# Memory attention in a decoder-trunk kernel: query weights loaded in one go, sample tokens queried with the second chunk, and their attention moved between the other slots

## The chip, the cores and the metric

The kernel runs as one program on 1 core of one Trainium2 chip. The metric is the device time of one execution in microseconds (us). The engines are TensorE (PE, with its weight loads, PEld), VectorE (DVE), ScalarE (ACT), GpSimd (POOL) and SyncE (SP), whose queue issues nearly all the DMAs here.

## The reference

One inference step of a decoder layer for 1,024 prompt tokens and 8 x 4 = 32 sample tokens, in three residual parts: a mixer (gated MLP beside latent attention), attention into a memory, and a gated feed-forward part with a short convolution. The change lies in the second part:

```python
def mem_attend(h, mk, mv, w_mq, g_mq, w_mo):
    n, t, _ = h.shape
    q = rms_norm((h @ w_mq).reshape(n, t, MEM_HEADS, MEM_HEAD_DIM), g_mq)
    s = jnp.einsum('nthd,nmhd->nhtm', q, mk.astype(q.dtype)).astype(jnp.float32) * (MEM_HEAD_DIM ** -0.5)
    p = jax.nn.softmax(s, axis=-1).astype(q.dtype)
    o = jnp.einsum('nhtm,nmhd->nthd', p, mv.astype(q.dtype)).reshape(n, t, MEM_WIDTH)
    return o @ w_mo
```

There are 4 heads of 128 and 256 memory tokens. The prompt attends to keys and values that the kernel computed earlier (`o_mk`, `o_mv`). Each of the 8 samples attends to its own cached keys and values, `mkT` and `mv` (8 tiles of 512 KB each), which are read from memory.

## The kernel before

Products are made three times over: an operand is split into a high and a low part (`split`: an ACT cast, then a DVE subtraction, lines 201 and 202, or 205 and 208 with a gain), and `mm3` (line 186) adds high x high, high x low and low x high.

**Output projection** (`out_proj`). Eight row tiles `m` by three token chunks of 384, 384 and 288. The last chunk holds 256 prompt tokens and the 32 sample tokens and runs two tiles late. Each result is added to the residual on DVE (line 1768), stored, split into `xh` and `xl` (the operand of the next stage) and squared (ACT), and the squares are summed on POOL (line 1801). After the last tile, `token_roots` makes the inverse token norms `r3` from the sums, by some twenty small DVE instructions per chunk.

**Memory attention** (`mem_attention`). PE's order is written out by hand (`manual_schedule`). For the other engines a scheduler makes the order when the program is built; at run time every engine takes its instructions strictly in that order. The work of PE is a list of slots `s`:

- `project(h)` loads the query weights of head `h` (`w_mq`, 512 KB) into one of three `raw` buffers, scales them on POOL (line 1576) and splits them: heads 0 to 2 into one of three pairs that the output projection also uses, head 3 into a pair of its own (`wxh`, `wxl`). `memory()` loads `o_mk` and `o_mv` through the same `raw` buffers and splits them into `kh`, `kl`, `vh` and `vl`. In the code the order is: project 0, slot 0, memory, project 1, slot 1, project 2, and so on.
- Slots 0 to 15 run over four chunks of 256 prompt tokens with four heads each. A slot is `scores` of five slots ago, `query`, `values` of seven slots ago and `trans` of six slots ago, each named for what it multiplies or transposes. A query writes one of two banks `b`; a bank is free again when DVE has made `ql` from it. The fourth chunk has 288 columns: the sample tokens come last, and the query makes `qs` (DVE) and `qm` (POOL) from them. Every fourth slot ends with `square_sums`, and `roots` follows one slot later.
- Slots 16 to 22 run the pipeline empty and hold the samples' attention: `sample_scores` with three, three and two samples in slots 16 to 18 (line 1930), a softmax, `sample_trans` in slot 19, `sample_values` with four samples each in slots 21 and 22 (line 1966), `sample_out` at the end. `ahead` (slots 19 to 22) makes the first pieces of the output product with `w_mo`. Keys and values of the samples go through five buffers `skT`; five keys are loaded ahead, and each further load is issued when a buffer has been used. The masks `pm` for the values are POOL products (line 1949) with four buffers.

After slot 15 the space of `xh` and `xl` is given to other tiles: four residual tiles (line 2029) and the sums of feed-forward weights (line 2241) are loaded there. After slot 22 comes the rest of the output product (tile `y`) and the feed-forward part.

Of the kernel before, what the change touches and what calls it, by code (L numbers as in the profile page):

```python
# [13 lines left out]
P = 128  # L14
# [140 lines left out]
class Net:  # L155
# [1648 lines left out]
    def mem_attention(self, xh, xl, r3):  # L1804
# [30 lines left out]

        def query(h, c):
            o, n = 256 * c, 288 if c == 3 else 256
            ps = bank("b", 2)[:, :n]
            self.mm3(ps, [(w[h][0][:, k], w[h][1][:, k]) for k in range(8)], [(xh[:, k, o : o + n], xl[:, k, o : o + n]) for k in range(8)])
            qsq[h] = self.t(p, [P, 288], F32, f"qsq{h}", 1)[:, :n]  # L1840
            nc.scalar.activation(qsq[h], ps, AF.Square)
            self.split(qh[:, h, o : o + n], ql[:, h, o : o + n], ps, gmq)
# [4 lines left out]
        rows = self.t(p, [P, 384], F32, "rows", 1)  # L1847

        def square_sums(c):

            n = 288 if c == 3 else 256
            st = bank("st", 1)[:, :n]
            for h in range(4):
                nc.tensor.matmul(st[32 * h : 32 * h + 32], self.ones[:, :32], qsq[h], start=True, stop=True)
            if c == 3:
                nc.gpsimd.memset(rows[:, n:], 1.0)
            nc.scalar.copy(rows[:, :n], st)

        def roots(c):

            m, t = 3 if c == 3 else 2, slice(2 * c, 9 if c == 3 else 2 * c + 2)
            st = bank("st", 1)[:, : m * P].rearrange("p (k n) -> p k n", k=m)
            for k in range(m):
                nc.tensor.transpose(st[:, k], rows[:, k * P : k * P + P], self.ident)
            x = self.t(p, [P, 3, 4], F32, "rsq", 2)[:, :m]
# [6 lines left out]

        units = [(h, g) for g in range(4) for h in range(4)]

        def scores(i):
            h, g = units[i]
            ps = bank("s", 2).rearrange("p (e n) -> p e n", e=2)
# [3 lines left out]
            pr[i] = self.t(p, [P, 2, 256], F32, "pr", 3)  # L1881
            self.softmax(p, pr[i], ps, P, rm[:, 2 * g : 2 * g + 2, h])

# [9 lines left out]
        def values(i):  # L1893
            h, g = units[i]
            th, tl = ts.pop(i)
# [28 lines left out]
        def sample_scores(b0, b1):  # L1924
# [7 lines left out]
            if b1 == NB:  # L1932
                sc = self.t(pe, [P, 1], F32, "sc")
                for h in range(4):
                    nc.gpsimd.tensor_copy(sc[heads[h]], rm[:NS, 8, h : h + 1])
                sample["p"] = self.t(pe, [P, 1, 256], F32, "pf", 1)
                self.softmax(pe, sample["p"], sample["s"].unsqueeze(1), P, sc)

        def sample_trans():
            tp = bank("st", 1)[:, :256].rearrange("p (k n) -> p k n", k=2)  # L1940
            for k in range(2):
                nc.tensor.transpose(tp[:, k], sample["p"][:, 0, k * P : k * P + P], self.ident)
            pT = self.t(pe, [P, 1, 256], F32, "pf", 1).rearrange("p a (k n) -> p (a k) n", k=2)
            nc.vector.tensor_copy(pT, tp)
            sample["m"] = []
            for b in range(NB):
                pm = self.t(pe, [P, 2, 4, NS], F32, "pm", 4)
                sample["m"].append(pm)
# [3 lines left out]
                )  # L1952
                if b < 4:
                    f()
# [3 lines left out]
        def sample_values(b0):  # L1958
            if b0 == 0:
                sample["o"] = bank("sx", 1)[:, :P]  # L1960
            so = sample["o"]
            for b in range(b0, b0 + 4):
                v, pm = skv.pop(0), sample["m"][b]
                for k in range(2):
                    for h in range(4):
                        nc.tensor.matmul(
                            so[heads[h]], pm[:, k, h], v[:, k, h * P : h * P + P], start=b + k == 0, stop=b == NB - 1 and k == 1
                        )
                if b0 == 0:
                    sample_load(1)  # L1970
                    sample["m", b + 4]()
            if b0:
                sample["d"] = self.t(pe, [P, 1, 256], F32, "pf", 1)[:, 0, :P]
                nc.scalar.copy(sample["d"], so)
# [25 lines left out]
        form = lambda p, h, n: ops[h].__setitem__(n, [self.t(p, [P, 4, QT], FR, f"{n}{h}{q}") for q in "hl"])  # L2000
        E = mybir.EngineType
        with tc.manual_schedule(engines={E.PE}):
            for s in range(16):
                if s < 4:
                    project(s)
                slot(s)
                if s == 0:
                    self.token_roots(p, bank("sx", 1), r3, 2)
                    nc.vector.tensor_copy(rt, r3)
                    memory()  # L2010
                if s == 7:
                    sample_load(5)
            self.close("x")
# [578 lines left out]
```

## Time and profile before

| | us |
|---|---|
| Runs shown: median (lowest to highest of 3) | 1833.23 (1832.74 to 1837.23) |
| The profiled execution: its own time | 1834.78 |
| Span of the profiled execution | 1833.0 |
| PE busy in the span | 1795.4 (98%) |
| DVE, ACT, POOL busy | 1353.7 (74%), 919.8 (50%), 713.2 (39%) |

The mean clock granted to TensorE was 0.992 of full speed. Times are counted from the start of the span. The output projection ends at about 981 us, the slots 0 to 15 lie between 983 and 1065 us, the slots 16 to 22 between 1065 and 1109 us, and the feed-forward part takes the rest. In a row of the timeline the columns are start, duration, engine, line, operation, tiles, count, and in brackets how long the engine was idle before and who ended that. A row of the chain of waits has start, duration and what. A row of the table of stretches has the stretch, its length, the busy time of each engine (with the number of instructions), the granted clock, the share of the DMA engines and GB/s.

### The profile page before, as it was taken

How to read it: one execution, taken by the hardware profiler on the slowest of the kernel's cores; microseconds unless marked ns; L12 is line 12 of the kernel's file. 1: busy time of each engine (PE TensorE's matmuls, PEld its weight loads, DVE VectorE, ACT ScalarE, POOL GpSimd, SP SyncE). 2: the span in 40 equal slices, each digit the busy share in tenths (PEclk: the TensorE clock that was granted, in tenths of full speed). 3: DMA queues.
4: the chain of work that ended last, by engine and by line, in shares of the span. 5: the costliest groups of instructions: out<-in, count | busy, mean ns of one | idle time of the engine just before them, and what ended most of it. 6: DMA issues, size and time to landing. Idle time of an engine off the chain costs nothing.

```text
span 1833.0 us, 39420 instructions
## 1 busy us (share of the span) xinstructions
PE 1795.4 (98%) x14259; PEld 1702.0 (93%) x14259; DVE 1353.7 (74%) x2805; ACT 919.8 (50%) x1921; POOL 713.2 (39%) x865
## 2 busy tenths in 40 slices
PE   9999999999999999999998989999999999999999
PEld 8999777779999999998897979999999999999999
DVE  7864767657678777788644676898888888888664
ACT  7435676766556555556433555533333333444442
POOL 1021655534445454553032021377667776400000
PEclk9999999999999999999998999999999999999999
DMA  8102354558776766663654065222222222495242
GB/s 322 46 18 72 123 164 127 167 181 232 211 208 183 202 183 189 181 194 124 186 156 163 13 215 174 83 82 79 95 72 71 82 71 82 144 331 163 83 149 78
DMA packets 153188, 261.19 MB, mean 142 GB/s; under 512 B 20897, under 2 KB 97538, under 8 KB 152994
## 3 DMA queue, kind: packets, MB, share of 16 engines
q1 hardware_dynamic: 152130, 257.63, 45.1%
q8 instruction: 113, 1.85, 0.4%
q10 hardware_dynamic: 864, 1.05, 0.2%
q14 instruction: 81, 0.66, 0.1%
HBM read 212.79 MB, written 45.82 MB: 141 GB/s over the span
## 4 chain that ended last, share of the span: by engine, by line
PE 80%; DVE 4%; ACT 2%; DMA 2%; issue 1%; SPq 0%; POOL 0%; DVEq 0%; ACTq 0%; POOLq 0%
PE s L186 22%; PE d L186 12%; PE b L186 8%; PE F L186 7%; PE X L186 7%; PE E L186 7%; PE A L186 3%; PE y L186 2%; PE o L1047 2%; PE o L1538 2%; PE tp L1032 1%; PE tp L186 1%; PE s L1423 1%; PE b L1606 1%; PE tp L985 1%
## 5 line engine op out<-in xcount | busy, mean ns | idle before, releaser
L186 PE MATMUL s<-w2h,ch 128*128 128x256 f32 x1018 | 302.3, 297 | 0.0
L186 PE MATMUL s<-w2h,cl 128*128 128x256 f32 x1018 | 293.7, 289 | 0.0
L186 PE MATMUL s<-w2l,ch 128*128 128x256 f32 x1018 | 293.3, 288 | 0.0
L186 PEld LDWEIGHTS s<-w2h,ch 128*128 128x128 f32 x1018 | 191.7, 188 | 3.3 <-issue 2.9
L186 PEld LDWEIGHTS s<-w2h,cl 128*128 128x128 f32 x1018 | 191.6, 188 | 0.4 <-DVE rqa L258 0.4
L186 PEld LDWEIGHTS s<-w2l,ch 128*128 128x128 f32 x1018 | 191.9, 189 | 0.0
L1459 DVE TENSOR_REDUCE ss<-sq 128x16 f32<-128x1024 f32 x128 | 155.3, 1213 | 28.9 <-ACT sq L1456 28.9
L1408 POOL TENSOR_TENSOR cl<-cT,ch 128x512 fp32r<-128x512 f32 x64 | 86.2, 1347 | 198.1 <-ACT ch L1404 183.8
L1456 ACT ACTIVATE sq<-s 128x512 f32<-128x512 f32 x128 | 76.4, 597 | 72.6 <-PE s L186 72.5
L201 ACT CAST a<-brb 128x528 fp32r<-128x528 f32 x77 | 48.8, 634 | 109.9 <-PE d L186 106.6
L1453 ACT ACTIVATE sq<-s 128x512 f32<-128x512 f32 x128 | 76.6, 599 | 50.0 <-PE s L186 38.2
L186 PE MATMUL d<-a,w 128*128 128x264 f32 x768 | 95.2, 285 | 0.0
L202 DVE TENSOR_TENSOR a<-brb,a 128x528 fp32r<-128x528 f32 x77 | 54.3, 707 | 54.8 <-ACT a L201 54.7
L186 PEld LDWEIGHTS d<-a,w 128*128 128x128 f32 x768 | 94.3, 189 | 0.0
L2228 POOL TENSOR_TENSOR lo<-s,hi 128x1024 fp32r<-128x1024 f32 x20 | 63.9, 3195 | 45.7 <-ACT hi L2227 45.7
L186 PE MATMUL mm<-wlo,xh 128*128 128x256 f32 (+3 forms) x272 | 77.2, 286 | 0.1
L186 PE MATMUL mm<-whi,xh 128*128 128x256 f32 (+3 forms) x272 | 77.2, 285 | 0.0
L186 PE MATMUL mm<-whi,xl 128*128 128x256 f32 (+3 forms) x272 | 77.0, 287 | 0.0
L2283 ACT COPY a<-A 128x264 f32<-128x264 f32 x43 | 16.1, 374 | 120.6 <-PE A L186 111.7
L1404 ACT CAST ch<-cT 128x512 fp32r<-128x512 f32 x128 | 73.6, 628 | 0.2 <-issue 0.2
L2349 POOL TENSOR_TENSOR cv<-cv,row 128x1056 f32<-128x1056 f32 x22 | 65.1, 2959 | 21.0 <-ACT cv L2348 21.0
L186 PE MATMUL d<-a,hi 128*128 128x264 f32 x552 | 72.0, 285 | 0.0
(800 smaller groups left out, 6401.4 us busy)
## 6 DMA issues: line engine op xcount, KB each, us to landing
cT<-cT SPq DMA_DIRECT2D x256, 160.0 KB, 2.6
ck<-ck SPq DMA_DIRECT2D x256, 144.0 KB, 3.5
raw<-w_up SPq DMA_DIRECT2D x44, 512.0 KB, 3.6
wsumd<-wsum SPq DMA_DIRECT2D x26, 512.0 KB, 3.6
actd<-cv SPq DMA_DIRECT2D x44, 264.0 KB, 2.3
brb<-actd SPq DMA_DIRECT2D x44, 264.0 KB, 5.6
wsum<-w_down SPq DMA_DIRECT2D x22, 512.0 KB, 3.7
raw<-wsumd SPq DMA_DIRECT2D x20, 512.0 KB, 3.8
```

Of the source, the lines that this page charges most:

```text
L186: x = self.nc.tensor.matmul(out, l, r, start=first and i == 0, stop=last and i == len(seq) - 1)
L201: first = {"act": nc.scalar.copy, "pool": nc.gpsimd.tensor_copy, "dve": nc.vector.tensor_copy}[eng](hi, src)
L202: low = lambda: nc.vector.tensor_tensor(lo, src, hi, ALU.subtract)
L1047: nc.tensor.matmul(u["o"][g : g + 64, o : o + m * P], s["v"][:, j, h % 4], th[:, z * P : (z + m) * P], start=j == 0, stop=b == len(banks) - 1,
L1404: nc.scalar.copy(d["h"][:, k], src[k])
L1408: (nc.vector if k else nc.gpsimd).tensor_tensor(d["l"][:, k], src[k], d["h"][:, k], ALU.subtract)
L1453: nc.scalar.activation(sq[:, 0], ps[:, :, n0 : n0 + 256], AF.Square)
L1456: nc.scalar.activation(sq[:, 1], pt.rearrange("p (e d) -> p e d", e=2), AF.Square)
L1459: yield lambda: nc.vector.tensor_reduce(s["ss"][:, g0 : g0 + 2].rearrange("p e (z h) -> p z e h", z=2), sq.rearrange("p z e (h d) -> p z e ...
L1538: nc.tensor.matmul(s["o"][j * 32 : j * 32 + 32], S[:, q * 4 + j], d["ck"][:, j, :257], start=q == 0 and j > 0, stop=q == 7)
L2228: eng.tensor_tensor(lo, src, hi, ALU.subtract)
L2349: nc.gpsimd.tensor_tensor(cv, cv, row, ALU.mult)
```

## The change

Three things are done, all between the output projection and the end of memory attention.

1. The query weights of all four heads are loaded first, then `memory()` and the first four sample keys; the slots follow.
2. The chunks are queried in the order 1, 0, 2, 3. In `xh` and `xl` the sample tokens stand first, so that chunk 0 has the 288 columns and is queried second, in slots 4 to 7. For this, `out_proj` splits the last chunk in two pieces: 256 columns and 32 columns, one more ACT cast and one more DVE subtraction for each of eight tiles. `rt`, `rows` and `rm` are ordered to match (four small copies in place of one).
3. The samples' scores go into slots 9 to 12 with two samples each, `sample_trans` into slot 14, the values into slots 16 to 19 with two samples each, `sample_out` into slot 20. There are four `skT` buffers and three `pm` buffers.

```diff
@@ out_proj, chunk
-            self.split(xh[:, m, o : o + n], xl[:, m, o : o + n], res)
+            w = min(NP_ - o, n)
+            self.split(xh[:, m, NS + o : NS + o + w], xl[:, m, NS + o : NS + o + w], res[:, :w])
+            if c == 2:
+                self.split(xh[:, m, :NS], xl[:, m, :NS], res[:, w:])
@@ mem_attention
+        order = (1, 0, 2, 3)
+        first = (0, 2, 5, 7)
-        def query(h, c):
-            o, n = 256 * c, 288 if c == 3 else 256
+        def query(h, i):
+            g = order[i]
+            o = 0 if g == 0 else NS + 256 * g
+            n, t = NS + 256 * (g + 1) - o, slice(256 * g, 256 * g + 256)
...
-            if c == 3:
-                nc.vector.tensor_scalar(qs[:, h], ps[:, 256:], gmq, None, ALU.mult)
+            if g == 0:
+                nc.vector.tensor_scalar(qs[:, h], ps[:, :NS], gmq, None, ALU.mult)
...
-                    skv.append(self.t(ps_, [P, 4, 256], F32, "skT", 5))
+                    skv.append(self.t(ps_, [P, 4, 256], F32, "skT", 4))
...
-                pm = self.t(pe, [P, 2, 4, NS], F32, "pm", 4)
+                pm = self.t(ps_, [P, 2, 4, NS], F32, "pm", 3)
...
+        SCORES = (9, 10, 11, 12)
         with tc.manual_schedule(engines={E.PE}):
+            for s in range(4):
+                project(s)
+            memory()
+            sample_load(4)
             for s in range(16):
-                if s < 4:
-                    project(s)
                 slot(s)
                 if s == 0:
                     self.token_roots(p, bank("sx", 1), r3, 2)
-                    nc.vector.tensor_copy(rt, r3)
-                    memory()
-                if s == 7:
-                    sample_load(5)
+                    for a, b, n in ((0, 2, 2), (2, 0, 2), (4, 8, 1), (5, 4, 4)):
+                        nc.vector.tensor_copy(rt[:, a : a + n], r3[:, b : b + n])
+                if s in SCORES:
+                    sample_scores(2 * SCORES.index(s), 2 * SCORES.index(s) + 2)
+                if s == 14:
+                    sample_trans()
...
             for s in range(16, 23):
                 if s < 21:
                     scores(s - 5)
-                if s < 19:
-                    sample_scores(3 * (s - 16), min(3 * (s - 15), NB))
-                elif s < 22:
-                    ahead(*divmod(s - 19, 2))
                 if s == 16:
                     roots(3)
-                if s == 19:
-                    sample_trans()
-                if s > 20:
-                    sample_values(4 * (s - 21))
-                if s == 22:
-                    ahead(1, 1)
+                if s < 20:
+                    sample_values(2 * (s - 16))
+                if s == 20:
+                    sample_out()
+                if s > 18:
+                    ahead(*divmod(s - 19, 2))
                 values(s - 7)
                 if s < 22:
                     trans(s - 6)
-            sample_out()
```

How the instructions stand at the places that the prediction speaks of (line numbers behind line 1767 are up to 14 higher in the changed kernel).

SP's queue around the end of the output projection, before: `raw` is a weight buffer, `skT` a sample buffer, `res_73` the stored residual.

```order
L1572 DMA raw_15924<-w_mq 128x1024
L1765 DMA res_15745<-xT 128x288
L1769 DMA res_73<-res_15711 128x288
L1572 DMA raw_15960<-w_mq 128x1024
L1769 DMA res_73<-res_15745 128x288
L1821 DMA blk_15849<-c_blkT 128x256
L1922 DMA skT_16258<-mkT 128x1024
...
L1922 DMA skT_16266<-mkT 128x1024
L1572 DMA raw_15996<-w_mq 128x1024
L1909 DMA raw_16874<-w_mo 128x512 x2
```

The same queue now:

```order
L1572 DMA raw_15897<-w_mq 128x1024
L1765 DMA res_15759<-xT 128x288
L1769 DMA res_73<-res_15723 128x288
L1834 DMA raw_15902<-o_mk 128x4x256
L1769 DMA res_73<-res_15759 128x288
L1834 DMA raw_15906<-o_mv 128x2x512
L1824 DMA blk_15865<-c_blkT 128x256
L1930 DMA skT_15910<-mkT 128x1024
...
L1930 DMA skT_15916<-mkT 128x1024
L1917 DMA raw_16969<-w_mo 128x512 x2
```

Between the two `skT` rows three more stood before, and two more stand now. The row at the top was the second of the four `w_mq` loads and is now the fourth; the last one stood behind the five `skT` loads. The two memory loads, which stood 12 and 5 rows ahead of the first piece, now come after the weights, ahead of the `skT` loads.

DVE between the last chunk of the output projection and the first `ql`, before (`rqx` reads a sum of squares from a PSUM bank, `lo`, `kl`, `vl` and `wxl` are low halves):

```order
L1768 TENSOR_TENSOR res_15745<-b_15747,res_15745 128x288
L247 TENSOR_SCALAR rqx_2300_15783<-o_15779 128x3
...
L202 TENSOR_TENSOR xl_14872<-res_15745,xh_14871 128x288
L247 TENSOR_SCALAR rqx_2305_15802<-m_15798 128x3
...
L247 TENSOR_SCALAR rqx_2336_15900<-sx_15896 128x3
L202 TENSOR_TENSOR kl_15841<-raw_15916,kh_15840 128x1024
...
L202 TENSOR_TENSOR vl_15843<-raw_15920,vh_15842 128x1024
...
L202 TENSOR_TENSOR lo_15963<-raw_15960,hi_15962 128x1024
L208 SCALAR_TENSOR_TENSOR ql_15839<-b_15867,gmq_15851,qh_15838 128x256
```

The same now:

```order
L1768 TENSOR_TENSOR res_15759<-b_15761,res_15759 128x288
L247 TENSOR_SCALAR rqx_2300_15799<-o_15795 128x3
...
L202 TENSOR_TENSOR lo_15893<-raw_15890,hi_15892 128x1024
...
L247 TENSOR_SCALAR rqx_2305_15818<-m_15814 128x3
L202 TENSOR_TENSOR xl_14872<-res_15759,xh_14871 128x256
L202 TENSOR_TENSOR xl_14872<-res_15759,xh_14871 128x32
...
L247 TENSOR_SCALAR rqx_2349_15951<-sx_15947 128x3
...
L202 TENSOR_TENSOR wxl_15861<-raw_15897,wxh_15860 128x1024
...
L202 TENSOR_TENSOR kl_15857<-raw_15902,kh_15856 128x1024
...
L202 TENSOR_TENSOR vl_15859<-raw_15906,vh_15858 128x1024
L208 SCALAR_TENSOR_TENSOR ql_15855<-b_15918,gmq_15867,qh_15854 128x256
```

Three long subtractions still stand between `rqx` of `sx` and the first `ql`; the third weight's `lo` now comes ahead of the reading of bank `m`.

SP's queue after slot 15, before (`s` are sums of feed-forward weights):

```order
L2029 DMA res_16866<-res_73 128x528
...
L2029 DMA res_16872<-res_73 128x528
L2241 DMA s_2660_17774<-wsumd_77 128x512 x2
L2241 DMA s_2661_17775<-wsumd_77 128x512
L1922 DMA skT_16917<-mkT 128x1024
L1922 DMA skT_16923<-mkT 128x1024
L1922 DMA skT_16929<-mkT 128x1024
L2241 DMA s_2661_17775<-wsumd_77 128x512
L1922 DMA skT_16993<-mv 128x1024
```

The same now:

```order
L2043 DMA res_16961<-res_73 128x528
...
L2043 DMA res_16967<-res_73 128x528
L2250 DMA s_2660_17792<-wsumd_77 128x512 x2
L2250 DMA s_2661_17793<-wsumd_77 128x512 x2
L1930 DMA skT_17038<-mv 128x1024
L1930 DMA skT_17049<-mv 128x1024
L1930 DMA skT_17095<-mv 128x1024
L1930 DMA skT_17106<-mv 128x1024
```

Two further `res` rows stand between the two shown, in both. The last three keys and all eight values came behind the residuals before; now the last four values do, and the other sample loads stand ahead of this piece.

More of the change, by code (lines that the diff above doesn't have):

```diff
@@ L1841, in query, with square_sums @@
             nc.scalar.activation(qsq[h], ps, AF.Square)
-            self.split(qh[:, h, o : o + n], ql[:, h, o : o + n], ps, gmq)
-            if c == 3:
-                nc.vector.tensor_scalar(qs[:, h], ps[:, 256:], gmq, None, ALU.mult)
+            self.split(qh[:, h, t], ql[:, h, t], ps[:, n - 256 :], gmq)
+            if g == 0:
+                nc.vector.tensor_scalar(qs[:, h], ps[:, :NS], gmq, None, ALU.mult)
                 nc.gpsimd.tensor_tensor(qm[h], blk, qs[:, h].unsqueeze(1).broadcast_to([P, NB, NS]), ALU.mult)
-        rows = self.t(p, [P, 384], F32, "rows", 1)
-        def square_sums(c):
-            n = 288 if c == 3 else 256
+        rows = self.t(p, [P, 288], F32, "rows", 1)
+        def square_sums(i):
+            n = 256 if order[i] else 288
             st = bank("st", 1)[:, :n]
@@ L1854, in square_sums, with roots @@
                 nc.tensor.matmul(st[32 * h : 32 * h + 32], self.ones[:, :32], qsq[h], start=True, stop=True)
-            if c == 3:
-                nc.gpsimd.memset(rows[:, n:], 1.0)
             nc.scalar.copy(rows[:, :n], st)
-        def roots(c):
-            m, t = 3 if c == 3 else 2, slice(2 * c, 9 if c == 3 else 2 * c + 2)
+        def roots(i):
+            at = [0, P] if order[i] else [NS, NS + P, 0]
+            m, t = len(at), slice(first[i], first[i] + len(at))
             st = bank("st", 1)[:, : m * P].rearrange("p (k n) -> p k n", k=m)
-            for k in range(m):
-                nc.tensor.transpose(st[:, k], rows[:, k * P : k * P + P], self.ident)
+            for k, a in enumerate(at):
+                nc.tensor.transpose(st[:, k], rows[:, a : a + P], self.ident)
             x = self.t(p, [P, 3, 4], F32, "rsq", 2)[:, :m]
@@ L1871, in roots @@
             nc.vector.tensor_tensor(rm[:, t], x, r, ALU.mult)
-        units = [(h, g) for g in range(4) for h in range(4)]
+        units = [(h, i) for i in range(4) for h in range(4)]
         def scores(i):
-            h, g = units[i]
+            h, i0 = units[i]
+            g, t0 = order[i0], first[i0]
             ps = bank("s", 2).rearrange("p (e n) -> p e n", e=2)
@@ L1881, in scores @@
             pr[i] = self.t(p, [P, 2, 256], F32, "pr", 3)
-            self.softmax(p, pr[i], ps, P, rm[:, 2 * g : 2 * g + 2, h])
+            self.softmax(p, pr[i], ps, P, rm[:, t0 : t0 + 2, h])
         def trans(i):
@@ L1893, in values @@
         def values(i):
-            h, g = units[i]
+            h, g = units[i][0], order[units[i][1]]
             th, tl = ts.pop(i)
@@ L1932, in sample_scores @@
             if b1 == NB:
-                sc = self.t(pe, [P, 1], F32, "sc")
+                sc = self.t(ps_, [P, 1], F32, "sc")
                 for h in range(4):
-                    nc.gpsimd.tensor_copy(sc[heads[h]], rm[:NS, 8, h : h + 1])
-                sample["p"] = self.t(pe, [P, 1, 256], F32, "pf", 1)
-                self.softmax(pe, sample["p"], sample["s"].unsqueeze(1), P, sc)
+                    nc.gpsimd.tensor_copy(sc[heads[h]], rm[:NS, 4, h : h + 1])
+                sample["p"] = self.t(ps_, [P, 1, 256], F32, "pf", 1)
+                self.softmax(ps_, sample["p"], sample["s"].unsqueeze(1), P, sc)
         def sample_trans():
@@ L1961, in sample_values @@
             so = sample["o"]
-            for b in range(b0, b0 + 4):
+            for b in range(b0, b0 + 2):
                 v, pm = skv.pop(0), sample["m"][b]
@@ L1968, in sample_values @@
                         )
[L1969 removed]
+                if b < 4:
                     sample_load(1)
[L1971 to L1973 removed]
+                if b < 5:
+                    sample["m", b + 3]()
+            if b0 == 6:
+                sample["d"] = self.t(ps_, [P, 1, 256], F32, "pf", 1)[:, 0, :P]
                 nc.scalar.copy(sample["d"], so)
```

4 lines of the change are left out of this document (2 added, 2 removed).

## The prediction

> **What bounds the kernel now.** I read the page first, then the table of stretches around the change, then PE's timeline there, and the chain of waits for how long the same matmuls take at different places.
>
> ```profile
> span 1833.0 us, 39420 instructions
> PE 1795.4 (98%) x14259; PEld 1702.0 (93%) x14259; DVE 1353.7 (74%) x2805; ACT 919.8 (50%) x1921; POOL 713.2 (39%) x865
> ```
>
> ```profile
> 983.00:1010.30 27.30, 19.67 (x137) 17.92 (x137) 11.83 (x39) 6.87 (x13) 4.40 (x4) 0.81 0.51 187
> 1043.17:1065.26 22.09, 21.98 (x179) 20.71 (x178) 17.98 (x57) 14.62 (x37) 2.30 (x4) 1.00 0.24 77
> 1063.55:1109.07 45.52, 38.01 (x411) 32.40 (x410) 26.07 (x75) 19.46 (x50) 10.23 (x15) 0.93 0.69 245
> 1200.00:1300.00 100.00, 100.00 (x824) 100.00 (x823) 87.06 (x109) 35.06 (x45) 69.37 (x51) 1.00 0.25 81
> ```
>
> PE is the bound nearly everywhere: in 1200 to 1300, a piece of the feed-forward part, it is busy for 100 of 100 us. Whatever attention gains, that part starts earlier by as much, and nothing there takes it back. Inside attention PE has losses in two stretches, 983 to 1010 (19.67 busy of 27.30, granted clock 0.81) and 1063 to 1109 (38.01 of 45.52, 0.93). In the slots between them it waits for nothing, and DVE has 17.98 of 22.09 filled. PE's timeline names the waits:
>
> ```profile
> 991.09 0.39 PE L186 MATMUL b<-xh,hi 128*128 128x256 f32 x1 [1.60 <-DVE ql L208]
> 999.74 0.58 PE L186 MATMUL b<-xh,wxh 128*128 128x256 f32 x1 [5.56 <-ACT wxh L201]
> 1001.00 0.58 PE L186 MATMUL b<-xh,wxl 128*128 128x256 f32 x1 [0.47 <-DVE wxl L202]
> 1074.19 0.64 PE L1930 MATMUL sx<-skT,qm 128*32 128x256 f32 x8 [3.16 <-DMA skT<-mkT]
> 1099.09 0.64 PE L1966 MATMUL sx<-skT,pm 128*32 128x128 f32 x16 [1.52 <-POOL pm L1949]
> 1102.22 0.99 PE L1966 MATMUL sx<-skT,pm 128*32 128x128 f32 x16 [2.48 <-DMA skT<-mv]
> 1103.48 1.08 PE L1966 MATMUL sx<-skT,pm 128*32 128x128 f32 x16 [0.27 <-DMA skT<-mv]
> ```
>
> Behind the longer waits the same matmuls take longer than elsewhere, as the granted clock says. From the chain of waits, in pairs of a slow and a full-speed piece (`st` x8 is `square_sums`, `t` x4 `trans`, `t` x6 `values`, `s` x6 `scores`, `b` x24 a query or a piece of the output product, `sx` x64 four samples' values):
>
> ```profile
> 1001.00 5.06 PE b L186 x22
> 1006.06 1.20 PE st L1854 x8
> 1011.24 2.83 PE b L186 x24
> 1023.46 0.57 PE st L1854 x8
> 1074.83 1.36 PE t L186 x6
> 1077.05 1.28 PE s L186 x6
> 1084.94 0.71 PE t L186 x6
> 1085.65 0.44 PE t L1889 x4
> 1086.09 0.72 PE s L186 x6
> 1090.88 2.90 PE b L186 x24
> 1093.77 1.88 PE sx L1966 x64
> 1104.56 3.67 PE b L186 x24
> ```
>
> So there are three losses.
> - Weights: 1.60 + 5.56 + 0.47 of waiting, then 22 matmuls in 5.06 instead of 2.59 (22 of 24 x 2.83) and `st` 1.20 instead of 0.57: 7.63 + 3.10 = 10.7 us.
> - Sample keys: 3.16, then 1.36 - 0.71 and 1.28 - 0.72: 4.4 us.
> - Sample values: 1.52 + 2.48 + 0.27, then 0.99 - 0.64, 1.08 - 0.64 and 3.67 - 2.90: 5.8 us.
>
> **Part 1, the weights first.** SP's row, POOL's, and two of DVE's:
>
> ```profile
> 988.25 0.33 SPq L1572 DMA_DIRECT2D raw<-w_mq  x1
> 996.71 1.89 POOL L1576 TENSOR_TENSOR raw<-raw,cols 128x1024 f32<-128x1024 f32 x1 [10.63 <-DMA raw<-w_mo]
> 989.42 1.22 DVE L202 TENSOR_TENSOR lo<-raw,hi 128x1024 fp32r<-128x1024 f32 x1
> 990.56 0.48 DVE L208 SCALAR_TENSOR_TENSOR ql<-b,gmq,qh 128x256 fp32r<-128x256 f32 x1
> ```
>
> Head 3's weights were issued at 988.25, when DVE had emptied a buffer of the memory's, and behind five sample loads. POOL waited 10.63 for them (the row puts the name of a later load in the same tile), then scaled, ACT and DVE split, PE stood. Now these weights come into a buffer that an earlier weight leaves about one tile ahead of the slots, so the 5.56, the 0.47 and their slow clock go. Their scaling and splitting runs beside out_proj's matmuls, as that of heads 0 and 1 did.
>
> Two things stay. By the order DVE still has three long subtractions (about 1.2 each) between the reading of `sx` and the first `ql`, which frees the bank for the third query, so the 1.60 stays. And head 2's `lo`, 1.22, now stands ahead of the reading of bank `m`, which the first query waits for: between 0 and 1.2 later, part of which the third query's wait takes up; I take 0.4. Part 1 gives 10.7 - 1.6 - 0.4 = **8.7**.
>
> The new danger is `o_mv`. Its buffer is now freed by that `lo`, and ACT has the cast to `vh` ahead of the first `qsq`. The output projection ends at 981; two splits of about 1.2 put the issue at 983.5. The load's own time before, and that of the five sample keys issued in 982 to 987:
>
> ```profile
> raw<-o_mv SPq DMA_DIRECT2D x1, 512.0 KB, 3.5
> ```
>
> ```profile
> DMA to landing us min/median/max: 8.5/9.6/10.5
> ```
>
> With 3.5 it lands at 987.0, and `vh` (about 1.1), `vl` and `ql` end at 989.8 at the earliest, inside the wait that stays. With 8.5 they end at 994.8, 3.7 behind the 991.09 of before. I take 3.5: it is issued ahead of the sample keys, and the equally spaced landings of the latter read like one transfer behind another.
>
> **Part 2, the samples queried with the second chunk.** PE's work is the same, 32 columns wider in slots 4 to 7 and not in 12 to 15. The eight more casts and subtractions lie under out_proj's matmuls. The samples' softmax now falls into slots 12 to 14 beside DVE's fullest stretch, and POOL's masks with it:
>
> ```profile
> L1949 POOL TENSOR_TENSOR pm<-pf,blk x8: 724/744/1192, 1085.7 to 1097.9; 128x256 f32<-128x256 f32 x8
> ```
>
> ```profile
> 1085.63 1.67 DVE L2216 TENSOR_SCALAR pr<-pr,rsum 128x256 f32<-128x256 f32 x2
> 1090.43 0.62 DVE L2216 TENSOR_SCALAR pr<-pr,rsum 128x256 f32<-128x256 f32 x2
> ```
>
> The same pair of DVE instructions took 1.67 while a mask ran and 0.62 otherwise. Three masks early in a row are 3 x 0.744 = 2.2 us of such blocking, against 4.1 us (22.09 - 17.98) of DVE's slack over about four slots and a pipeline of five slots from scores to values. I take **-0.3**, between 0 and -2.2. The Trainium skill, "SBUF — State Buffer", section "SBUF: two separate sides", calls the port pair that DVE and GpSimd share an exclusive lock held for a whole instruction, and so speaks against this placing; the trace agrees (1.67 against 0.62), and were nothing of it hidden, the sum would be 2.2 lower instead of 0.3.
>
> **Part 3, the end.** The keys' loss (4.4) goes, since all keys are used by slot 12, and the values' (5.8), since four values and the masks are there early. But the last four values come behind the loads that follow slot 15's query:
>
> ```profile
> 1060.36 3.19 PE b L186 x24
> 1063.59 1.75 SPq L2029 DMA_DIRECT2D res<-res  x4
> 1065.38 1.38 SPq L2241 DMA_DIRECT2D s<-wsumd  x3
> 1066.95 1.37 SPq L1922 DMA_DIRECT2D skT<-mkT  x3
> ```
>
> ```profile
> DMA to landing us min/median/max: 8.0/8.4/8.8
> ```
>
> Call X the end of slot 15's query (1060.36 + 3.19 = 1063.55). Four `res` and now four `s` are issued ahead (1.75 + 4/3 x 1.38), so value 4 goes out at X + 3.7; the buffer is free by then (value 0 is used up at about X + 3.1). The comparable key went out at 1066.95 and ended PE's wait at 1074.19: 7.2. So value 4 is there at X + 10.9. PE asks for it after the rest of slot 15 (0.71 + 0.44 + 0.57), slot 16 (0.72 + about 0.2 for the roots + 0.94 for two samples + 0.71 + 0.44), slot 17 (0.72 + 0.94 + 0.71 + 0.44) and the scores of slot 18 (0.72): X + 8.3. It waits 2.6. Value 5 lands some 0.9 behind value 4 (0.46 of issue and 0.4 by the spread of the landings) and is wanted 0.47 behind: 0.4 more. A slow stretch follows; behind the two late losses it cost 1.2 and 1.6, I take 1.4. New loss 4.4, part 3 gives 4.4 + 5.8 - 4.4 = **5.8**.
>
> The slow clock is itself disputed. PE kept its speed after 1.60 (0.39 for the first matmul, and 2.83 for a query later), but the matmul after 2.48 took 0.99 instead of 0.64. The Trainium skill, "TensorE: Matmul & The Clock Gate", section "Why this matters for your kernels", says "No PE-idle gaps >~3µs between matmul bursts"; the 2.48 here speaks against so late a bound. By that rule the 2.6 and 0.4 would cost no clock, and the sum would be 1.4 more, 15.6 (the first rival).
>
> **Sum:** 8.7 - 0.3 + 5.8 = 14.2. The profiled execution took 1834.78 (span 1833.0 and 1.78 around it), 1.55 over the median. From 1834.78 it comes to 1820.6, from the median 1833.23 to **1819.0**.
>
> **Rivals.** A measurement of this kernel tells about 0.3% (5.5 us) from no change.
> - *PE keeps its speed behind the wait at the end.* Gain 14.2 + 1.4 = 15.6, 1817.6. For it: no slow row behind 1.60. Against: those behind 2.48. It is the case that the Trainium skill's rule above would give.
> - *The end does not wait.* If value 4 lands as `o_mv` did, in 3.5, it is there at X + 7.2, ahead of X + 8.3. Gain 14.2 + 4.4 = 18.6, 1814.6. For it: three key loads less in that stretch. Against: res and s, which stood ahead of the keys that took 7.2, still stand there.
> - *The end waits long.* With 10.5, the longest landing shown, value 4 is there at X + 14.2: 5.9 + 0.4 of waiting, and a slow stretch like that behind the weights, 3.1: 9.4 in place of 4.4. Gain 9.2, 1824.0.
> - *The memory's values are late.* With 8.5 for `o_mv` the third query starts 3.7 later and slowly (1.4): gain 14.2 - 5.1 = 9.1, 1824.1.
> - *Both of these.* Gain 4.1, 1829.1: no difference that could be told.
> - *Slower: four buffers are too few.* Keys 4 to 7 and values 4 to 7 are each issued only when a buffer has been used, two slots ahead of their use. A slot with samples is 2.83 + 0.72 + 0.71 + 0.44 + 0.94 = 5.6, so slots 11 and 12 wait from a landing of 11.3 on. At 16 they wait 2 x 4.7 and run slowly after (2 x 1.4), and the end waits 11.4 + 0.4 + 3.1 in place of 4.4: 14.2 - 12.2 - 10.5 = -8.5, 1841.7. It would be slower by 5.5 from about 15 on. Against: no landing over 10.5 is shown, and the DMA engines are 24% busy in those slots.
> - *The change does not do what it says.* The order speaks against that: head 3's weights stand ahead of the sample keys, and only four values behind slot 15.
>
> **How the numbers follow.** Forecast 0.47 (its own range, with 8.7 + 0.4 or less 0.8, masks 0 to -2.2 and clock 0 to 3.1: 1817 to 1823). Speed kept 0.10. No wait at the end 0.14. Long wait 0.12. Values late 0.09. Both 0.04. Slower 0.04. Faster is the sum of the first five, 0.92; same 0.04; slower 0.04. The range takes in the first five: below, no wait at the end with the 1.60 gone as well and 1 for other sizes, 1812; above, the two late cases and 1 more, 1825.
>
> **What would show it.** In the profile after, PE must have no wait for `wxh` or `wxl` and one of 1 to 2 us for `ql` at the third query; no wait for `mkT`; in slots 4 to 15 at most 1 us in all; one wait of 2 to 4 us for `mv` ahead of value 4, followed by `s` or `t` groups over 1 us. POOL's last `w_mq` scaling must stand ahead of 981. I am wrong if the third query waits for `vh`, if PE waits for `pr` or `th` around slots 13 to 16, or if the feed-forward part does not move up by what attention gains.

## The result and the profile after

The changed kernel takes 1818.70 us (median of 4 runs, 1818.34 to 1820.74) against 1833.74 before (4 runs, 1832.74 to 1837.23): a ratio of 0.9917, 95% interval 0.9900 to 0.9934. That is 15.0 us less; the forecast was 14.2 less, 1819.0. The profiled execution took 1818.99. The total is right, and in part by luck: part 1 gave 2.1 less than forecast and parts 2 and 3 together 2.8 more, and these errors nearly cancel.

The page after, its span and PE, and the same four kinds of rows of the table of stretches:

```profile
span 1817.3 us, 39434 instructions
PE 1789.8 (98%) x14259; PEld 1697.7 (93%) x14259; DVE 1356.3 (75%) x2816; ACT 921.5 (51%) x1929; POOL 712.6 (39%) x864
```

```profile
983.00:1010.30 27.30, 24.99 (x189) 23.88 (x189) 15.30 (x69) 8.87 (x22) 1.94 (x3) 0.94 0.48 167
1043.17:1065.26 22.09, 21.22 (x211) 19.32 (x210) 19.06 (x59) 14.46 (x39) 2.56 (x4) 1.00 0.60 191
1200.00:1300.00 100.00, 100.00 (x824) 100.00 (x823) 90.27 (x111) 33.62 (x44) 73.69 (x59) 1.00 0.26 81
```

PE is now busy for 24.99 of the first 27.30 us, where it had 19.67, and the feed-forward piece is full as before. PE's waits in the whole of memory attention, by what was waited for (total, number, longest), from the view of the waits after:

```profile
PE b L186 <- DVE rqx L247: 1.9, 1, 1.9
PE b L186 <- DVE ql L208: 1.5, 1, 1.5
PE sx L1974 <- DMA skT<-mv: 1.0, 2, 0.6
PE t L186 <- DVE c L2038: 0.9, 1, 0.9
PE t L186 <- DVE tl L202: 0.8, 1, 0.8
```

Before, this list had 5.6 for `wxh`, 3.2 for `mkT`, 2.8 for `mv`, 1.6 for `ql`, 1.5 for `pm`, 0.5 for `rqx`, 0.5 for `wxl` and 0.3 for `pr`. Those for `wxh`, `wxl`, `mkT`, `pm` and `pr` have gone and the one for `mv` is down to 1.0. The first in the new list has grown from 0.5, and the last two are new.

To see what each part gave, I cut both traces at four places: the first sum `o` behind the output projection, the start of the fifth query, the end of slot 15's query, the first output product `y`. After, from PE's timeline:

```profile
980.52 0.72 PE L296 MATMUL o<-ones,acc 128*128 128x1 f32 x6
...
1000.09 0.40 PE L186 MATMUL b<-xh,hi 128*128 128x288 f32 x1
...
1059.85 0.28 PE L186 MATMUL b<-xh,wxl 128*128 128x256 f32 x1
...
1093.42 0.39 PE L186 MATMUL y<-qh,hi 128*128 128x264 f32 x1
```

The third row is the last matmul of slot 15's query, so that one ends at 1060.13. Before, the four places were at 981.04, 1007.19, 1063.55 and 1108.82. The same cut through the experiments (us between the places; "before o" is the time up to the first place):

| | before o | o to fifth query | to end of slot 15's query | to first y | from y on |
|---|---|---|---|---|---|
| before | 981.04 | 26.15 | 56.36 | 45.27 | 724.18 |
| changed | 980.52 | 19.57 | 60.04 | 33.29 | 723.88 |
| weights_only | 980.09 | 20.92 | 56.38 | 44.11 | 724.20 |
| samples_only | 981.20 | 24.71 | 60.04 | 32.92 | 724.03 |
| after_again | 984.78 | 19.61 | 60.03 | 32.91 | 723.87 |
| lo_behind | 979.20 | 16.47 | 60.03 | 32.26 | 723.94 |
| banks | 981.65 | 16.96 | 60.03 | 32.59 | 723.87 |
| filler | 979.77 | 16.82 | 60.04 | 32.43 | 723.84 |
| mem_behind | 979.28 | 14.64 | 60.03 | 32.75 | 724.10 |
| sums_behind | 981.64 | 21.08 | 60.04 | 32.25 | 723.89 |
| trans13 | 980.32 | 18.31 | 60.07 | 32.62 | 723.88 |
| both | 979.70 | 14.64 | 60.04 | 32.19 | 724.03 |
| both_trans13 | 980.72 | 14.63 | 60.05 | 31.37 | 724.13 |

Each row is one execution. The stretch ahead of `o`, in which PE's work is the same in all these kernels, differs by up to 5.6 us between executions (979.20 to 984.78), and by 4.3 between two of the changed kernel (changed and after_again); their spans, 1817.3 and 1821.2, differ by no more than that. So small effects are read from the other columns. The last column is the same within 0.4: what attention gains is passed on whole.

Part 1 lies in the second column: 26.15 - 19.57 = 6.6 instead of the 8.7 of the prediction. Parts 2 and 3 lie in the third and fourth: 101.63 - 93.33 = 8.3 instead of 5.8 - 0.3 = 5.5. (The third column grows by 3.7, since the samples' scores and transposes moved into it from the fourth.)

What failed in part 1 is seen in the chain of waits after, from the end of the sums to the fifth query:

```profile
981.73 1.23 DVE lo L202
982.96 0.68 DVE rqy L249
983.63 0.07 DVE rqx L247
983.70 0.14 issue
983.84 4.34 PE b L186 x24
988.18 0.57 PE sx L296 x6
...
991.56 1.13 DVE vl L202
992.69 0.41 DVE ql L208
993.10 0.04 issue
993.14 5.92 PE b L186 x48
999.07 1.09 PE st L1862 x8
```

Head 2's `lo` stands in front, then `rqx` reads the bank, and only then does the first query begin; and that query takes 4.34, where it took 3.04 before (982.95 to 985.99).

### The profile page after: what moved, and what is told of

The parts are those of the page before. It is cut to its first block, busy times and chain, and to the rows that moved or that the text cites. A ratio compares the mean times of both kernels' runs of the same rounds, so it can differ in the third digit from the quotient of the medians.

```text
span 1817.3 us, 39434 instructions
## 1 busy us (share of the span) xinstructions
PE 1789.8 (98%) x14259; PEld 1697.7 (93%) x14259; DVE 1356.3 (75%) x2816; ACT 921.5 (51%) x1929; POOL 712.6 (39%) x864
## 4 chain that ended last, share of the span: by engine, by line
PE 81%; DVE 4%; ACT 1%; issue 1%; POOL 1%; DMA 1%; SPq 0%; DVEq 0%; POOLq 0%; ACTq 0%
PE s L186 23%; PE d L186 12%; PE b L186 8%; PE F L186 7%; PE X L186 7%; PE E L186 7%; PE A L186 3%; PE y L186 2%; PE o L1047 2%; PE o L1538 2%; PE tp L1032 1%; PE tp L186 1%; PE s L1423 1%; PE tp L985 1%; PE v L186 1%
```

## The experiments

All times are against runs of the kernel before on the same chip; where only the profile can tell, the columns above are used.

**One part at a time.** weights_only is the kernel before with this edit:

```diff
+            for s in range(4):
+                project(s)
+            memory()
+            sample_load(5)
             for s in range(16):
-                if s < 4:
-                    project(s)
                 slot(s)
                 if s == 0:
                     self.token_roots(p, bank("sx", 1), r3, 2)
                     nc.vector.tensor_copy(rt, r3)
-                    memory()
-                if s == 7:
-                    sample_load(5)
```

> The kernel before with part 1 alone: the four query weights, the memory's loads and five sample keys ahead of the slots. Theory (part 1 is worth what the two traces show up to the fifth query, 26.05 - 19.48 = 6.6 us, because head 2's subtraction now delays the first query by 1.4 and leaves it at half clock for 1.5): 6 to 7 us faster than before. Rival (the prediction's sum for part 1 holds, and the rest is lost elsewhere): 8.7 faster.

Measured: 1827.46 against 1834.46, ratio 0.9958 (0.9943 to 0.9974), 7.0 us by the medians. The interval, 4.8 to 10.5 us, holds both expectations, so the columns decide. In the second one it gained 26.15 - 20.92 = 5.2, and its first query took 5.45. So the 8.7 is not there when the part stands alone either; the theory's 6.6 is nearer. Another 1.2 lie in its fourth column, where the waits for `mv` were 1.7 instead of 2.8.

samples_only is the changed kernel with that edit undone (four sample keys loaded behind slot 7).

> The changed kernel with part 1 undone: weights, memory and first sample keys are issued where they were before; chunk order and sample placement are the new ones. Theory (parts 2 and 3 are worth 8.5, since the wait at the end is 1.0 instead of 3.0 and costs no clock): 8 to 9 us faster than before, and together with weights_only about 15. Rival (the prediction's sum, 5.8 - 0.3): 5.5 faster.

Measured: 1824.10 against 1834.46, ratio 0.9941 (0.9928 to 0.9954), 10.4 by the medians, more than both expected. Its third and fourth columns gained 101.63 - 92.96 = 8.7, as the theory said. The rest is in the second, 1.4: four sample keys instead of five stand ahead of head 3's weights there, they landed 5.6 after their issue instead of 8.3, and PE's wait for them fell from 5.6 to 3.1; a slow first query, 4.58 instead of 3.04, took part of that back. The two results do not simply add (7.0 + 10.4 is more than 15.0). By the columns the second one does (5.2 + 1.4 against 6.6), though with a first query of another speed in each; most of the excess is the 1.2 of weights_only in the fourth column, which the samples' new places take away anyway.

**Undoing the one subtraction.** lo_behind:

```diff
...
-            w[h] = self.stream(I["w_mq"][h], 8, "g_mem_x", hl=hl)
+            self.lows = [] if h == 2 else None
+            w[h] = self.stream(I["w_mq"][h], 8, "g_mem_x", hl=hl)
+            if h == 2:
+                self.behind(self.lows.pop()(), self.rqx)
+                self.lows = None
```

Here `self.rqx` is the instruction that reads bank `m`, and `behind` orders one instruction behind another of its engine. after_again is the changed kernel once more.

> The changed kernel as it is, so that the others of this group stand beside it on the same chip. Both theories: 15 us faster than before; the first query again waits 1.9 for the reading of bank m and takes 4 us or more instead of 2.8 if the half clock comes from that wait each time.

> The changed kernel with one subtraction moved: the low half of head 2's weights is ordered behind the reading of bank m on DVE. Theory (this one instruction is what the prediction priced at 0.4 and what cost 2.9): the first query waits about 0.5 and takes 2.8, and from the sums to the fifth query it takes about 16.7 instead of 19.6: 2.9 us faster than the changed kernel. Rival (the start of the stage costs this much wherever the subtraction stands): within 1 us of the changed kernel.

Measured: after_again 1819.98 against 1832.73, ratio 0.9919 (0.9900 to 0.9938), with the wait of 1.94 and a first query of 4.36 again; lo_behind 1813.67, ratio 0.9892 (0.9872 to 0.9911). The second column went from 19.61 to 16.47, 3.1 less, where 2.9 was expected: 1.6 of waiting ahead of the first query, 1.3 of its slow clock and 0.2 of the third query's wait. (By the medians it is 6.3 below after_again; the intervals overlap.) DVE's timeline of lo_behind:

```profile
979.95 0.16 DVE L247 TENSOR_SCALAR rqx<-o 128x3 f32<-128x3 f32 x1
...
980.62 0.16 DVE L247 TENSOR_SCALAR rqx<-m 128x3 f32<-128x3 f32 x1
980.77 0.42 DVE L202 TENSOR_TENSOR xl<-res,xh 128x256 fp32r<-128x256 f32 x1
981.10 1.22 DVE L202 TENSOR_TENSOR lo<-raw,hi 128x1024 fp32r<-128x1024 f32 x1
```

The read of `m` now comes 0.67 behind that of `o`; in the changed kernel 2.27 lay between them. The first query starts at 980.93, 0.34 of waiting ahead of it, and takes 3.06. So the place of this one subtraction is the cause of the 1.4 that the first query waits longer.

**The same wait removed in two other ways.** banks hands the PSUM banks out in another order, so that the first query does not write where `m` stands; DVE's order is the same as in the changed kernel, row for row. filler lets PE work in the gap.

```diff
-        for tag in "bst":
+        for tag in "stb":
             bank(tag, 2)
```

```diff
             sample_load(4)
+            fill = bank("t", 2)[:, :256]
+            for k in range(16):
+                nc.tensor.matmul(fill, w[0][0][:, k % 8], xh[:, k % 8, 288:544], start=True, stop=True)
             for s in range(16):
```

> The changed kernel with the PSUM banks handed out in another order, so that no query writes the bank of the sums m; everything else as it is. Theory (the first query waits for the reading of bank m behind head 2's subtraction): its wait of 1.93 falls below 0.5 and it runs at full clock, 2.8 instead of 4.3; the wait of the third query grows from 1.5 to about 2.4, because DVE's chain behind the sums sx sets it; 2.5 us faster than the changed kernel, 17.5 faster than before. Rival (DVE's subtractions set the third query's start whatever the first does): within 0.5 of the changed kernel.

> The changed kernel with 16 extra matmuls of 256 columns, whose result nobody reads, between the sums m and the first query, in the time in which PE waits. Theory (the first query runs at half clock because PE did next to nothing for 3.2 us): the first query takes 2.8 instead of 4.3, 1.5 us faster than the changed kernel, 16.5 faster than before. Rival (the granted clock there has another cause than idle time): no gain, the first query stays at 4.3.

Measured: banks 1816.02 against 1834.46, ratio 0.9898 (0.9883 to 0.9913); filler 1814.25, ratio 0.9894 (0.9877 to 0.9912). In the second column 19.57 became 16.96 (2.6 less, 2.5 expected) and 16.82 (2.8 less, 1.5 expected). In both the first query runs at full speed. From the tables of stretches, the first 2.5 us of it in the changed kernel, in banks and in filler (the number ahead of the last two is the granted clock):

```profile
983.84:986.34 2.50, 2.50 (x12) 2.50 (x13) 2.35 (x23) 1.05 (x1) 0.00 (x0) 0.50 0.78 234
```

```profile
982.90:985.40 2.50, 2.50 (x23) 2.50 (x23) 2.50 (x8) 2.03 (x5) 1.08 (x1) 1.00 1.00 264
```

```profile
983.02:985.52 2.50, 2.50 (x23) 2.50 (x22) 2.43 (x24) 1.05 (x1) 0.00 (x0) 1.00 0.77 211
```

In the same 2.50 us PE got through 12 matmuls at a clock of 0.50 and through 23 at 1.00. In banks the third query's wait for `ql` grew to 2.21, as expected, and no slow stretch followed. filler gained more than its theory said because its DVE order is another one: `wxl` and `kl` come ahead of the reading of `sx`, and the third query no longer waits at all. The first query of filler kept its clock, as its theory has it. But in trans13 (below) it kept its clock as well, after a wait of 1.93 and without any filler, so this one profile does not show that the extra matmuls did it; and the gain beyond that is not an answer to the question filler was made for.

**The third query's wait.** mem_behind is banks with this beside it:

```diff
...
-                self.split(hi.rearrange("p h n -> p (h n)"), lo.rearrange("p h n -> p (h n)"), raw)
+                hi, lo = (x.rearrange("p h n -> p (h n)") for x in (hi, lo))
+                self.behind(nc.scalar.copy(hi, raw), q1[0])
+                self.behind(nc.vector.tensor_tensor(lo, raw, hi, ALU.subtract), q1[1])
```

`q1` holds the `qh` and `ql` instructions of the latest query, here the second, since `memory()` and the loads of the first four sample keys now stand behind slot 1.

> The kernel called banks, and beside it the splitting of the memory's keys and values ordered behind the second query's on ACT and DVE. Theory (the wait of the third query is made of the three long subtractions ahead of the first ql): that wait falls from 2.2 to below 0.5, 2 us faster than banks, 4.5 faster than the changed kernel. Rival (the keys and values are then late for slots 5 to 7): the wait comes back there as a wait for kh, kl or vl, no gain over banks.

Measured: 1814.02 against 1832.73, ratio 0.9897 (0.9879 to 0.9914). The second column is 14.64, 2.3 less than in banks, and PE has no wait left in it; none for `kh`, `kl` or `vl` comes later. The median alone could not have told: by medians it lies 18.7 below before, banks 18.4.

**The end.** sums_behind orders the loads of `s` behind the last value load; trans13 moves the samples' transposes.

```diff
...
-                nc.sync.dma_start(s[:, k : k + 4].rearrange("p k n -> p (k n)"), self.wsum_dram[:, NK + sums, i, j])
+                x = nc.sync.dma_start(s[:, k : k + 4].rearrange("p k n -> p (k n)"), self.wsum_dram[:, NK + sums, i, j])
+                if sums == 0:
+                    self.behind(x, self.mv)
```

```diff
-                if s == 14:
+                if s == 13:
                     sample_trans()
```

`self.mv` is the latest load into a sample buffer, here the last value.

> The changed kernel with the four loads of feed-forward sums ordered behind the last four value loads on SP's queue. Theory (the waits for values 4 and 5, 0.4 + 0.65, come from the loads ahead of them): value 4 is issued about 1.8 earlier and both waits go, 1.0 us faster than the changed kernel, and nothing in the feed-forward part waits for the sums. Rival (the transfers share the engines' rate, so the order on the queue does not matter): the waits stay, no gain.

> The changed kernel with the samples' transposes, and the masks behind them, one slot earlier (13 instead of 14). Theory (the wait of 0.87 behind slot 15's query is DVE held up by the copy to pf and by three masks on POOL while it scales pr): that wait falls below 0.3 and no wait of the size comes one slot earlier, because there the masks do not meet a weight split on DVE; from the fifth query to the start of the output product 0.6 us less, about 0.5 us faster than the changed kernel, which the timing can hardly tell. Rival (the masks hold up DVE wherever they stand): a wait of 0.5 to 0.9 in slot 14, no gain.

Measured: sums_behind 1816.87 against 1832.73, ratio 0.9908 (0.9890 to 0.9926); trans13 1817.23 against 1833.61, ratio 0.9914 (0.9900 to 0.9927). Neither can be told from the changed kernel by time. In the fourth column sums_behind is 1.0 below the changed kernel and 0.7 below after_again, and PE has no wait for `mv` any more. But lo_behind and filler, whose queue was not touched there, had none either: in profiles of this queue that wait was 0 to 1.2. trans13 lost the 0.87 wait behind slot 15's query, no new one came a slot earlier, and the wait for `mv` stood at 1.2 instead of 1.0 and 0.6:

```profile
1067.04 0.39 PE L186 MATMUL t<-tl,vh 128*128 128x256 f32 x1 [0.76 <-DVE tl L202]
1069.61 0.64 PE L1974 MATMUL sx<-skT,pm 128*32 128x128 f32 x16 [0.55 <-DMA skT<-mv]
```

```profile
1070.90 0.65 PE L1974 MATMUL sx<-skT,pm 128*32 128x128 f32 x16 [0.64 <-DMA skT<-mv]
```

So its 0.87 came back in part as waiting for the load.

**Together.** both is mem_behind and sums_behind; both_trans13 has the transposes in slot 13 too.

> The bank order, the memory's splitting behind the second query, and the sums' loads behind the values, together. Theory (the gains lie in separate places and add): 14.6 us from the sums to the fifth query and 32.3 behind slot 15's query; 5.5 us faster than the changed kernel, 20.5 faster than before. Rival (an earlier start makes the end wait for the values or the feed-forward part for the sums): no faster than mem_behind.

> The kernel called both, with the samples' transposes one slot earlier as well. Theory: 0.6 us faster than both by the profile's stages. Rival: the same as both, with the wait one slot earlier.

Measured: 1812.45 and 1812.32 against 1833.61, both with a ratio of 0.9877 (0.9861 to 0.9894, and 0.9860 to 0.9894). The expected columns are met: 14.64 and 32.19, and with the transposes 31.37, 0.8 less, now that no load waits behind them. By time both is 21.2 below the kernel before (20.5 expected); the changed kernel was 15.0 and 12.8 below it in the two other groups. Against mem_behind the intervals overlap. By their medians these are the fastest kernels of this study.

## Why the prediction was right, and where it was not

The way of the change and its size were forecast, but two of the terms behind them were mis-sized. Of the prediction's own signs, these came: no wait for `wxh`, `wxl` or `mkT`, 1 to 2 us for `ql` at the third query, at most 1 us in slots 4 to 15, and a feed-forward part that moves up by what attention gains. The wait of 2 to 4 us for `mv` with a slow stretch behind it did not come. And in slot 15 PE waited 0.87 for `tl`, the low half of what `trans` made, which is close to its sign of being wrong ("if PE waits for `pr` or `th` around slots 13 to 16").

**Loss 1 went.** No wait for `wxh` or `wxl` is left, POOL's last scaling of weights ends ahead of 981, and it lies under out_proj's matmuls:

```profile
972.03 1.90 POOL L1576 TENSOR_TENSOR raw<-raw,cols 128x1024 f32<-128x1024 f32 x1 [3.14 <-DMA raw<-w_mq]
```

**The third query's wait stayed,** 1.47 for the 1.60 forecast, and for the reason given: mem_behind took it away by moving two of the three subtractions.

**o_mv was in time.** It was issued at 982.98 and landed in 4.3, between the 3.5 taken and the 8.5 feared. ACT waited 2.29 for it, ahead of the first `qsq`, with no loss to PE:

```profile
987.26 1.05 ACT L201 CAST vh<-raw 128x1024 fp32r<-128x1024 f32 x1 [2.29 <-DMA raw<-o_mv]
988.22 0.38 ACT L1849 ACTIVATE qsq<-b 128x256 f32<-128x256 f32 x1
```

**The step that failed in part 1** is "between 0 and 1.2 later, part of which the third query's wait takes up; I take 0.4". The place was right and the size was not. The wait ahead of the first query went from 0.51 to 1.93, more than the 1.22 of the subtraction: behind it `rqy` took 0.68 on the chain (0.76 in the timeline, where rows overlap), where such a step takes 0.17, and the read of `m` came after that. (An `xl` of 0.36, which stood ahead of that read before, now stands behind it.) `rqy` ended together with POOL's last addition to the squares:

```profile
982.87 0.76 DVE L249 TENSOR_SCALAR rqy<-rqy 128x3 int32<-128x3 int32 x1
982.54 1.06 POOL L1804 TENSOR_TENSOR acc<-acc,sqx 128x288 f32<-128x288 f32 x1 [2.09 <-ACT sqx L1803]
```

The same pair ended together in banks (984.77 and 984.75) and in filler (982.91 and 982.88). So the subtraction seems to have pushed `rqy` under that addition, where POOL held DVE up as in part 2 below; no run takes the two apart, since lo_behind moved `rqy` ahead of the addition as well. The third query's wait took up nothing, since the chain to it starts from the sums `sx`, which PE makes behind the first query. And the prediction had no term for the clock there: 4.34 - 3.04 = 1.3. Together 2.7, against 0.4: the whole shortfall of part 1, less the 0.1 by which the third query's wait shrank. lo_behind took back 3.1 by moving that one instruction. Two smaller mistakes cancel. The 22 slow matmuls of loss 1 leave out the first two of that query, slow as well (999.74 to 1001.00), which gave 0.55 more. The other one went the way of the shortfall: of the slow rows of loss 1, `st` with 1.20 did not recover. It takes 1.09 after, at a granted clock of 1.00, because it needs ACT's fourth `qsq` (999.10 to 999.48); it was in large part a wait, read as a slow clock.

**Part 2 cost 0.87 where 0.3 was forecast.** In slots 4 to 15 PE waited once, behind slot 15's query. (Its row names `c`, a small memset; the matmul reads `tl`, which ended just ahead of that, at 1061.06.) The blocking is seen again: the pair of DVE instructions took 1.17 at 1059.29, while three masks ran on POOL from 1057.91 to 1060.05, and the next pair 0.62:

```profile
1059.29 1.17 DVE L2225 TENSOR_SCALAR pr<-pr,rsum 128x256 f32<-128x256 f32 x2
...
1061.19 0.62 DVE L2225 TENSOR_SCALAR pr<-pr,rsum 128x256 f32<-128x256 f32 x2
```

The trace agrees here too with the exclusive lock of the Trainium skill's page "SBUF — State Buffer", section "SBUF: two separate sides". trans13 shows the price of this placing: at most the 0.87, of which the copy to `pf`, moved with the masks, may be a part.

**The step that failed in part 3** is "It waits 2.6", with the 0.4 and the 1.4 behind it. PE waited 0.38 and 0.65, and no slow stretch followed:

```profile
1061.11 0.39 PE L186 MATMUL t<-tl,vh 128*128 128x256 f32 x1 [0.87 <-DVE c L2038]
...
1069.31 0.39 PE L186 MATMUL t<-tl,vh 128*128 128x256 f32 x1 [0.76 <-DVE tl L202]
```

```profile
1071.71 0.65 PE L1974 MATMUL sx<-skT,pm 128*32 128x128 f32 x16 [0.38 <-DMA skT<-mv]
1073.00 0.65 PE L1974 MATMUL sx<-skT,pm 128*32 128x128 f32 x16 [0.65 <-DMA skT<-mv]
```

Value 4 was there at 1071.71, 11.6 behind the end of slot 15's query; 10.9 was forecast. (It was issued at 1065.10, 5.0 behind, since the four `res` took 2.95 on the queue and not 1.75.) But PE asked for it only at 1071.33, 11.2 behind and not 8.3: two waits for DVE, 0.87 and 0.76, lay in front, and the rest, 1.3, is that a slot takes longer than the sum of its rows (`scores` is 0.72 at its best and 0.90 behind another tile). The forecast compared a full landing time with a bare sum of work; the load was covered by delays that cost something themselves. The wait of 0.76 is for `tl` again: the small steps of `roots` ahead of it on DVE took 0.70, 0.66 and 0.68, where such steps took 0.17 beside them, while pairs of the values' masks ran on POOL (1064.84 to 1066.27 and 1067.90 to 1069.31). No run took these masks away. The new loss is 0.87 + 0.76 + 0.38 + 0.65 = 2.7 instead of 4.4 and 0.3. Another 0.7 of the 2.8 by which parts 2 and 3 did better would be two rows that the prediction counted in no loss: 0.85 instead of 0.44 for four transposes behind the wait for keys, and 0.3 for `pr` in slot 14. That sum is not closed row by row: a wait of 0.35 for `pr` in slot 6 went too, and `scores` behind the samples' tiles lost some.

**The rivals.** "PE keeps its speed behind the wait at the end" came true as far as the end goes, though the wait was also shorter; the others did not happen. The rule of the Trainium skill behind it ("TensorE: Matmul & The Clock Gate", section "Why this matters for your kernels") would give no loss of clock at the end, and so it was. At the start it would give none either, counting the wait of 1.93 alone; there the trace differs, unless the sums of one column count as idle too. With them PE did 1.31 us of work in the 3.20 ahead of the slow query:

```profile
980.60:983.80 3.20, 1.31 (x13) 1.22 (x11) 3.01 (x9) 2.73 (x5) 1.06 (x1) 0.92 0.61 213
```

## What to carry to other kernels

Where a load is moved ahead, follow what it triggers: its casts and subtractions arrive earlier as well, and here one of them, 1.2 us long, landed in front of a 0.16 us instruction on which the next stage hung. A bank or buffer that the first instruction of a stage happens to inherit can matter as much as its data; handing out the banks in another order was worth 2.6 us. And before a landing time is set against the work ahead of it, add the waits that lie in that work, for they cover each other: removing one alone shows the next.

## What the hardware showed that was not expected

The half clock behind a short gap came and went with nearly the same wait ahead of it. Behind 1.93 to 2.01 ahead of the first query, 12 or 13 of its matmuls were slow in the two profiles of the changed kernel, all 24 in weights_only and sums_behind, and none in trans13, whose order is that of the changed kernel up to there:

```profile
983.64:986.14 2.50, 2.50 (x21) 2.50 (x22) 2.35 (x23) 1.05 (x1) 0.00 (x0) 1.00 0.89 247
```

In samples_only PE waited only 0.57, ran seven matmuls at full speed and then fifteen slow ones, the slow ones beginning 0.9 us behind the start of the query:

```profile
983.93 0.28 PE L186 MATMUL b<-xh,hi 128*128 128x256 f32 x1
984.05 0.34 PE L186 MATMUL b<-xl,hi 128*128 128x256 f32 x1
984.19 0.41 PE L186 MATMUL b<-xh,lo 128*128 128x256 f32 x1
984.40 0.42 PE L186 MATMUL b<-xh,hi 128*128 128x256 f32 x1
```

The waits of 1.47 and 2.21 ahead of the third query were never followed by one. So the length of the last wait does not decide; what does, the runs leave open. That 1.3 to 2.4 us hang on it is shown by the first query's 4.34 and 5.46 against 3.07. It may be one reason why executions of one kernel differ, but the two profiles of the changed kernel agree there (4.34 and 4.36).
